# Copies of the weight sums moved from SyncE's queue to GpSimd's, each tied by a one-element transfer to a unit of the mLSTM's projection

## The chip, the cores and the metric

The kernel runs on one core of a Trainium2 chip. The core has five engines, each with its own in-order queue of instructions: PE (TensorE, matmuls), DVE (VectorE), ACT (ScalarE), POOL (GpSimd) and SP (SyncE). In this kernel SP and POOL issue all transfers, and sixteen DMA engines carry out those of both. The metric is device time in microseconds (us) of one execution.

## What is computed

One layer of a transformer-like trunk for 64 sample rows and 1024 prompt rows of width 1024, in float32:

```python
mod = silu(c) @ w_ada + b_ada                     # 48 blocks of 128 columns: shifts, scales, gates
u = rmsnorm(x, norm1_g) * (1 + sc1) + sh1
proj = u @ w_in                                   # q, k, v, mq, mk, mv, mo, gates
y_a = stick_breaking_attention(q, k, v)           # 8 heads x 64
conv = silu(depthwise_conv4(mq, mk))              # its last 3 inputs are an output, conv_new
y_b = sigmoid(mo) * norm(mlstm(conv, mv, mi, mf)) # 4 heads x 128
x = x + g1 * ((sigmoid(ga)*(y_a @ w_a) + sigmoid(gb)*(y_b @ w_b)) @ w_out)
u2 = rmsnorm(x, norm2_g) * (1 + sc2) + sh2
x = x + g2 * ((silu(u2 @ w_ff_gate) * (u2 @ w_ff_up)) @ w_ff_down)
y = rmsnorm(x, final_g)
```

## The kernel before

Every float32 operand is split into a high and a low part, and each product is three matmuls (`mm3`, lines 76 to 78). For a weight block, `w_unit` loads 128 columns (`wr`, line 64, 512 KB, on SP), and POOL makes the two parts (`hi_pool`, line 53, and `lo_pool`, line 59). `wr`, `wh` and `wl` have three buffers each.

**Start.** SP loads x and the first weights. `ada_pair(kb)` loads two blocks of `w_ada` (`wada`, line 212, ten buffers, 512 KB each), PE multiplies them (line 215) and transposes the result (line 220), and DVE makes `mod` and `A1` of it (line 238). `make_u(kb)` then scales `xnT[kb]` on ACT (line 299), POOL makes `uh` and DVE `ul`, and PE adds the slice `kb` to the first two units of the projection (`ps_mx`: mq and mk of head 0). This happens for kb = 0 to 7, so that 16 blocks of `w_ada` are needed before the first unit of the projection is done. Then come the gates' matmuls (`ps_if`, lines 573 and 574) and the units mv and mo of head 0.

**The mLSTM phase.** For each head h = 0 to 3 the list `dense` has the units q, k, v of the attention and mq, mk, mv, mo of head h + 1 (for h = 3 blocks of `w_ada` and gates in their place), and `run` weaves the steps of `mlstm(h)` between them. At the end of an mq or mk unit, `evac_x` copies six columns into the small tile `cvo` (lines 685 and 686), which is written out as `conv_new` at the end of the phase. Column b of `cvo` belongs to block b: blocks 0 to 3 are mq of heads 0 to 3, blocks 4 to 7 are mk. POOL also makes the value tiles `vst`, the mask sums of `W` (line 728), `hsq` (line 784) and the product at the end of the convolution (line 698) here.

**The weight sums.** The gate and up products of ten of the 22 blocks of the FFN use sums of quarters of `w_ff_gate` and `w_ff_up`, which are prepared in DRAM: four tensors `wsum_d[1]` to `wsum_d[4]`, each 512 x 1280. Each is made by a copy of one summand (`sum_copy`, two halves of 1280 KB, DRAM to DRAM) and an accumulating transfer of the other (`sum_add`, two halves, on POOL). Sum 2 adds sum 1, and sum 4 adds sum 2. They are read by the FFN stage (`load_pair`, line 1270).

**The order of the work.** The code runs within a framework that records all instructions with their dependences and then orders each engine's queue with its own simulated timeline: an instruction can be put ahead of those that stand before it in the program as soon as nothing that it depends on is open. Waits are semaphores, and each engine's queue is fixed at build time. A DMA that writes what an earlier DMA wrote, or reads what an engine writes, waits for it in the queue of the engine that issues it.

Of the kernel before, what the change touches and what calls it, by code (L numbers as in the profile page):

```python
# [35 lines left out]
def trunk(ctx, tc, a, o, dbg=None, stop=None):  # L36
    nc = tc.nc
# [82 lines left out]
    cvo = const.tile([P, 48], F32, name="cvo")  # L120
# [32 lines left out]
    NFC = NF * P  # L153
    wsum_d = {x: dram.tile([KH, NFC], F32, name=f"wsum{x}_d") for x in (1, 2, 3, 4)}
    g1w, g2w, u1w, u2w = w_g[0:KH, 0:NFC], w_g[KH:D, 0:NFC], w_u[0:KH, 0:NFC], w_u[KH:D, 0:NFC]
    sum_parts = {1: (u1w, u2w), 2: (g1w, wsum_d[1]), 3: (u1w, g1w), 4: (g2w, wsum_d[2])}

    def sum_copy(x):
        def go():
            for c in range(0, NFC, NFC // 2):  # L160
                nc.sync.dma_start(wsum_d[x][:, c : c + NFC // 2], sum_parts[x][0][:, c : c + NFC // 2])
            return
            yield
        return go()

    def sum_add(x):
        def go():
            for c in range(0, NFC, NFC // 2):
                nc.gpsimd.dma_start(wsum_d[x][:, c : c + NFC // 2], sum_parts[x][1][:, c : c + NFC // 2], accum_op=ALU.add)
            return  # L170
            yield
        return go()
# [644 lines left out]
    def qkv_units(p):  # L817
        return [in_unit(f"q{p}", OFF_Q + P * p, (p, 0), evac_qk, alloc_qk),
                in_unit(f"k{p}", OFF_K + P * p, (p, 1), evac_qk, alloc_qk), k_post(p),
                in_unit(f"v{p}", OFF_V + P * p, (p,), evac_v, alloc_v), v_post(p)]  # L820

    def ml_units(h):
        return [in_unit(f"mq{h}", OFF_MQ + P * h, (h, 0), evac_x, alloc_x),
                in_unit(f"mk{h}", OFF_MK + P * h, (h, 1), evac_x, alloc_x),
                in_unit(f"mv{h}", OFF_MV + P * h, (h,), evac_mv, alloc_mv),
                in_unit(f"mo{h}", OFF_MO + P * h, (h,), evac_mo, alloc_mo)]
# [8 lines left out]
    def chain(gens):  # L835
        for g in gens:
            yield from g

    def run(consumer, dense, nsteps, nd):

        n = 0.0
        done = False
        if nd == 0:
            for _ in consumer:
                pass
            done = True
        for _ in dense:
            n += nsteps / max(nd, 1)
            while n >= 1.0 and not done:
                n -= 1.0  # L850
                done = next(consumer, "end") == "end"
        for _ in consumer:
            pass
# [52 lines left out]
    for h in range(4):  # L906
        q_, k_, kp, v_, vp = qkv_units(h)
        m_ = ml_units(h + 1) if h < 3 else ada_left[0:2] + gates[0:2]
        b_ = [[sum_copy(1), sum_copy(3), sum_copy(2), sum_copy(4)], [sum_add(1), sum_add(3)], [sum_add(2)], [sum_add(4)]][h]
        dense = []  # L910
        for i, g in enumerate([q_, k_, kp, v_, vp] + m_):
            dense += [g] + (b_[i // 2 : i // 2 + 1] if i % 2 == 0 else [])
        run(mlstm(h), chain(dense), 14, 23 if h < 3 else 17)
# [99 lines left out]
    for m in range(KB):  # L1013
        if m % 2 == 0:
            wh, wl = wide_unit(w_a, 0, 4, m // 2, f"wa{m}")
        for c, (s, e) in enumerate(CHUNKS):
# [11 lines left out]
            for lo, hi in ([(s, HT), (HT, e)] if s < HT < e else [(s, e)]):  # L1028
                h = lo // HT
# [535 lines left out]
```

## Time and profile before

| | us |
|---|---|
| median of 3 runs | 1891.38 |
| lowest and highest | 1888.59 and 1891.83 |
| profiled execution | 1888.55 |
| its span | 1886.8 |
| PE busy (share of the span) | 1766.3 (94%) |
| POOL busy | 664.6 (35%) |
| mean granted clock of TensorE | 0.969 |

The span is what the profiler recorded; the profiled execution took 1.75 us more than it. A row of the timeline gives the start, the duration, the engine, the line of the code, the operation, the tile written and the tiles read, the count and, in brackets, how long the engine was idle before and what ended that. A row of the waits gives who waited for what, the total in us, how many times, and the longest. "In" tensors are the kernel's inputs in DRAM. MB and GB/s are decimal.

### The profile page before, as it was taken

What the parts mean: (1) busy time and instruction counts of PE and PEld (TensorE: products, weight loads), DVE (VectorE), ACT (ScalarE), POOL (GpSimd) and SP (SyncE); (2) the same over time, 40 slices, a digit from 0 to 9 for tenths busy, and PEclk for the clock granted to TensorE, in tenths of its full rate; (3) what the DMA queues carried; (4) which work ended last, traced back from release to release, by engine and by line L of the source; (5) the groups of instructions that cost most, each with busy time, mean ns of one, the idle gap of its engine ahead of it and who ended that gap; (6) DMA issues with size and microseconds to landing.
All of it is one profiled execution on the core that took longest, in us unless ns stands there. A gap on an engine that the chain in (4) does not pass through costs nothing. (4 is left out here: it accounts for less than half of the span.)

```text
span 1886.8 us, 31673 instructions
## 1 busy us (share of the span) xinstructions
PE 1766.3 (94%) x12388; PEld 1701.0 (90%) x12388; DVE 1000.8 (53%) x1903; ACT 670.5 (36%) x1401; POOL 664.6 (35%) x546
## 2 busy tenths in 40 slices
PE   6459999999989999997998999999999999999997
PEld 4349999999989888886898999999999999999997
DVE  5242242424236857687755198755554676444535
ACT  4023243434224444444422267433332443100005
POOL 2233353535243322249566350032222002254333
PEclk9769999999999999998999999999999999999999
DMA  9985333233485556477467345732232566443102
GB/s 273 269 218 135 98 96 106 84 118 79 132 188 136 131 136 155 128 196 218 138 205 209 106 127 159 207 108 75 69 92 75 173 203 185 170 151 116 57 12 96
DMA packets 315224, 265.51 MB, mean 141 GB/s; under 512 B 13638, under 2 KB 285250, under 8 KB 315074
## 3 DMA queue, kind: packets, MB, share of 16 engines
q1 hardware_dynamic: 305218, 235.16, 42.0%
q0 software_dynamic: 9856, 28.32, 7.3%
q8 instruction: 98, 1.61, 0.3%
q14 instruction: 52, 0.43, 0.1%
HBM read 206.59 MB, written 77.81 MB: 151 GB/s over the span
## 5 line engine op out<-in xcount | busy, mean ns | idle before, releaser
L76 PE MATMUL ps_fd<-hh,wh_fd 128*128 128x384 f32 (+1 forms) x480 | 157.1, 327 | 1.2 <-DVE hst L1333 1.2
L78 PE MATMUL ps_fd<-hh,wl_fd 128*128 128x384 f32 (+1 forms) x480 | 157.2, 327 | 0.0
L77 PE MATMUL ps_fd<-hl,wh_fd 128*128 128x384 f32 (+1 forms) x480 | 157.1, 327 | 0.0
L56 DVE TENSOR_TENSOR w<-wr,w 128x512 fp32r<-128x512 f32 x140 | 95.4, 691 | 39.4 <-ACT w L47 36.4
L1417 DVE SCALAR_TENSOR_TENSOR x1f<-ps_fd,mod,x1f 128x384 f32<-128x384 f32 (+2 forms) x128 | 60.4, 496 | 101.8 <-PE ps_fd L78 101.8
L388 DVE TENSOR_TENSOR_SCAN re<-re 128x128 f32<-128x128 f32 (+3 forms) x64 | 107.3, 1679 | 13.3 <-ACT re L384 12.9
L47 ACT CAST w<-wr 128x512 fp32r<-128x512 f32 x140 | 85.1, 619 | 69.6 <-PE ps_gd L1341 17.7
L53 POOL TENSOR_SCALAR wh_fd<-wr_fd 128x1024 fp32r<-128x1024 f32 x20 | 24.6, 1232 | 227.6 <-PE ps_ga L1341 119.4
L76 PEld LDWEIGHTS ps_fd<-hh,wh_fd 128*128 128x128 f32 x480 | 90.1, 188 | 1.4 <-POOL wl_fd L59 1.4
L78 PEld LDWEIGHTS ps_fd<-hh,wl_fd 128*128 128x128 f32 x480 | 90.1, 188 | 0.0
L77 PEld LDWEIGHTS ps_fd<-hl,wh_fd 128*128 128x128 f32 x480 | 90.1, 188 | 0.0
L47 ACT CAST hh<-hr 128x1088 fp32r<-128x1088 f32 (+1 forms) x26 | 24.0, 961 | 175.2 <-PE ps_fd L77 152.3
L384 ACT ACTIVATE re<-z 128x512 f32<-128x512 f32 (+2 forms) x96 | 47.3, 494 | 91.0 <-DVE z L380 70.6
L1341 PE MATMUL ps_ga<-b1h,w 128*128 128x272 f32 x352 | 75.0, 292 | 2.5 <-ACT g L1326 1.8
L215 PE MATMUL ps_ada<-wada,cT 128*32 128x128 f32 x768 | 43.1, 309 | 33.8 <-DMA wada<-in_w_ada 33.5
L1341 PE MATMUL ps_gc<-b5h,w 128*128 128x272 f32 x352 | 74.7, 292 | 0.0
L1341 PE MATMUL ps_gb<-b6h,w 128*128 128x272 f32 x352 | 74.4, 290 | 0.2 <-ACT g L1326 0.2
L1341 PE MATMUL ps_gd<-b7h,w 128*128 128x272 f32 x352 | 74.4, 290 | 0.0
L1341 PE MATMUL ps_gc<-b3h,w 128*128 128x272 f32 x352 | 73.7, 288 | 0.0
L1341 PE MATMUL ps_gd<-b4h,w 128*128 128x272 f32 x352 | 73.6, 289 | 0.0
L1341 PE MATMUL ps_ga<-b2h,w 128*128 128x272 f32 x352 | 73.5, 288 | 0.0
L215 PEld LDWEIGHTS ps_ada<-wada,cT 128*32 128x32 f32 x768 | 23.2, 119 | 49.5 <-issue 26.5
(549 smaller groups left out, 6108.8 us busy)
## 6 DMA issues: line engine op xcount, KB each, us to landing
wada<-in_w_ada SPq DMA_DIRECT2D x48, 512.0 KB
wr<-wsum_d SPq DMA_DIRECT2D x80, 256.0 KB
h_d<-hst SPq DMA_DIRECT2D x44, 272.0 KB
wr<-in_w_ff_gate SPq DMA_DIRECT2D x40, 256.0 KB
wr_fd<-in_w_ff_down SPq DMA_DIRECT2D x20, 512.0 KB
hr<-h_d SPq DMA_DIRECT2D x18, 544.0 KB
wr_g<-in_w_ff_gate SPq DMA_DIRECT2D x12, 512.0 KB
wr_u<-in_w_ff_up SPq DMA_DIRECT2D x12, 512.0 KB
```

The costliest lines, as they stand in the source:

```text
L47: nc.scalar.copy(out, in_)
L53: nc.gpsimd.tensor_scalar(out, in_, 1.0, 0.0, ALU.mult, ALU.add)
L56: nc.vector.tensor_sub(out, in_, h.bitcast(F32))
L76: nc.tensor.matmul(ps, wh, xh, start=first, stop=False)
L77: nc.tensor.matmul(ps, wh, xl, start=False, stop=False)
L78: nc.tensor.matmul(ps, wl, xh, start=False, stop=last)
L215: nc.tensor.matmul(ps[g : g + 32, b * P : (b + 1) * P], cT[:, kb, :], raw[:, kb, :], start=kb < 4, stop=kb >= 4, tile_position=(0, g))
L384: nc.scalar.activation(rest[:, c0 : c0 + w], ps, AF.Sigmoid, scale=-scale)
L388: nc.vector.tensor_tensor_scan(r, r, r, 1.0, ALU.mult, ALU.bypass)
L1341: nc.tensor.matmul(ps, w[:, a, j, :], b[j // 2][:, j % 2, :], start=p in (1, 6, 5, 7) and j == 0 and k == 0, stop=j == 3 and k == 2, skip_ ...
L1417: nc.vector.scalar_tensor_tensor(x1[m][:, lo:hi], ps[:, lo - s : hi - s], mod[:, 40 + m, g : g + 1], x1[m][:, lo:hi], ALU.mult, ALU.add)
```

## The change

`sum_copy` takes a second argument, a column of `cvo`. Both halves of each copy are issued by POOL instead of SP, and ahead of each half a transfer of one element (4 bytes) from that column of `cvo` goes into the first element of the place that the half fills; the half then overwrites it. Copies 1 and 3 are tied to blocks 1 and 5 (mq and mk of head 1), copies 2 and 4 to blocks 2 and 6 (mq and mk of head 2). In the program, the copies move from the units of h = 0 to those of h = 1 and 2, and the accumulating transfers stand a few units later than they did. What is computed stays the same.

```diff
-    def sum_copy(x):
+    def sum_copy(x, b):
+
         def go():
             for c in range(0, NFC, NFC // 2):
-                nc.sync.dma_start(wsum_d[x][:, c : c + NFC // 2], sum_parts[x][0][:, c : c + NFC // 2])
+                nc.gpsimd.dma_start(wsum_d[x][0:1, c : c + 1], cvo[0:1, b : b + 1])
+                nc.gpsimd.dma_start(wsum_d[x][:, c : c + NFC // 2], sum_parts[x][0][:, c : c + NFC // 2])
             return
             yield
         return go()
...
         m_ = ml_units(h + 1) if h < 3 else ada_left[0:2] + gates[0:2]
-        b_ = [[sum_copy(1), sum_copy(3), sum_copy(2), sum_copy(4)], [sum_add(1), sum_add(3)], [sum_add(2)], [sum_add(4)]][h]
+        b_ = [[], [sum_copy(1, 1), sum_copy(3, 5), sum_add(1), sum_add(3)], [sum_copy(2, 2), sum_copy(4, 6), sum_add(2)],
+              [sum_add(4)]][h]
         dense = []
         for i, g in enumerate([q_, k_, kp, v_, vp] + m_):
             dense += [g] + (b_[i // 2 : i // 2 + 1] if i % 2 == 0 else [])
```

## The prediction

> **What bounds the kernel now.** I read the forty slices of the page first, for stages in which PE is not busy.
>
> ```profile
> PE   6459999999989999997998999999999999999997
> DMA  9985333233485556477467345732232566443102
> ```
>
> PE is at 9 nearly everywhere but in the first four slices (a slice is 47 us), where the DMA engines are at 9, 9, 8. So the start is bound by transfers and the rest by PE. The busy times by window then place it.
>
> ```profile
> 40.00:61.50 21.50, 19.13 (x172) 16.19 (x171) 10.41 (x17) 5.04 (x7) 14.14 (x11) 1.00 0.99 283
> 61.50:125.50 64.00, 21.05 (x142) 17.19 (x142) 7.70 (x23) 6.20 (x13) 7.15 (x7) 0.60 1.02 254
> 125.50:160.00 34.50, 30.57 (x183) 26.01 (x181) 22.07 (x48) 12.54 (x18) 17.39 (x10) 0.95 0.82 167
> ```
>
> After start and length come PE, PEld, DVE, ACT and POOL, then PE's clock, the DMA engines' share and GB/s. From 61.5 to 125.5 PE works 21.05 of 64 us, at a clock of 0.60, with the DMA engines full. The waits of PE from 51 to 120 name what it lacks.
>
> ```profile
> PE ps_ada L215 <- DMA wada<-in_w_ada: 32.8, 5, 17.8
> PE ps_mx L76 <- POOL uh L53: 11.1, 2, 8.8
> ```
>
> 32.8 us go to blocks of `w_ada`. The timeline of SP shows why they are late.
>
> ```profile
> 40.63 1.25 SPq L161 DMA_DIRECT2D wsum_d<-in_w_ff_up  x2
> 41.97 0.60 SPq L212 DMA_DIRECT2D wada<-in_w_ada  x1
> 42.62 5.43 SPq L161 DMA_DIRECT2D wsum_d<-in_w_ff_up  x1
> 48.15 1.12 SPq L212 DMA_DIRECT2D wada<-in_w_ada  x1
> 49.31 5.87 SPq L161 DMA_DIRECT2D wsum_d<-in_w_ff_up  x1
> 55.23 27.18 SPq L161 DMA_DIRECT2D wsum_d<-in_w_ff_gate  x4
> 82.51 6.54 SPq L64 DMA_DIRECT2D wr_mo<-in_w_in  x1
> 89.15 17.69 SPq L212 DMA_DIRECT2D wada<-in_w_ada  x3
> ...
> 108.65 1.58 SPq L212 DMA_DIRECT2D wada<-in_w_ada  x1
> ```
>
> All eight copies stand in SP's queue from 40.6 us, far ahead of their place in the program: nothing held them back. Issuing them alone takes 1.25 + 5.43 + 5.87 + 27.18 = 39.7 us (the transfers push back), and the last four blocks of `w_ada` are issued only from 89 on. The 11.1 us on `uh` come from the same place, as the timelines of POOL and PE show.
>
> ```profile
> 83.25 1.00 POOL L169 DMA_DIRECT2D wsum_d<-in_w_ff_gate  x1 [22.22 <-DMA wsum_d<-in_w_ff_up]
> 83.90 1.48 POOL L53 TENSOR_SCALAR uh<-xnT 128x1088 fp32r<-128x1088 f32 x1
> 85.44 1.28 PE L76 MATMUL ps_mx<-uh,wh_mq 128*128 128x320 f32 x3 [8.76 <-POOL uh L53]
> ```
>
> POOL stood 22.22 us in front of an accumulating transfer whose copy had not landed; `uh` was behind it, and PE behind `uh`.
>
> **The change part by part.**
>
> *The copies leave SP's queue at the start.* Will they stay out of it? Each half now overwrites an element that a one-element transfer writes, and that reads a column of `cvo`. These are the copies into columns 1 and 2; columns 5 and 6, of the mk units, are written after each.
>
> ```profile
> 213.19 1.16 DVE L685 COPY cvo<-xp 128x3 f32<-128x3 f32 x1 [2.78 <-ACT xp L678]
> ...
> 310.30 1.16 DVE L685 COPY cvo<-xp 128x3 f32<-128x3 f32 x1 [2.77 <-ACT xp L678]
> ```
>
> No copy can start before 213 us of today's timeline, and no accumulating transfer before its copy. So the start loses the eight copies and, with them, accumulating transfers such as that at 83 us.
>
> Do the DMA engines still bind? The rows of SP show the last six blocks of `w_ada` (1, 1, 3 and 1). From 40 us on these six and the weights of mv, mo and q are to be moved: 9 x 512 KB = 4.72 MB, and at the 283 GB/s of the window from 40 that is 16.7 us. The last block would land at about 57 us, before 61.5, where PE ran dry. So PE is next to bind. What it has left then is worked out from these rows.
>
> ```profile
> 58.83 0.64 PE L215 MATMUL ps_ada<-wada,cT 128*32 128x128 f32 x16
> 74.37 1.08 PE L215 MATMUL ps_ada<-wada,cT 128*32 128x128 f32 x16 [12.70 <-DMA wada<-in_w_ada]
> 122.42 0.65 PE L76 MATMUL ps_mx<-uh,wh_mq 128*128 128x320 f32 x3
> 125.53 0.31 PE L573 MATMUL ps_if<-uh,wif 128*16 128x320 f32 x1
> 51.63 0.38 PE L220 MATMUL ps_ada<-ident,ada_sb 128*128 128x128 f32 x2
> 54.32 0.77 PE L76 MATMUL ps_mx<-uh,wh_mq 128*128 128x320 f32 x3 [2.31 <-POOL uh L53]
> ```
>
> Five blocks at 0.64, three pairs of transposes at 0.38 and three slices of `ps_mx` at 125.53 - 122.42 = 3.11: 3.2 + 1.1 + 9.3 = 13.6 us at the full clock, where the window has 21.05 at 0.60. Not all of that will be gapless: in the five slices before, the one gap after 43 us was 2.31 us, for `uh`. For three slices I allow 4.4 us, two such gaps less a little. The stretch of 64 us then takes 18 us, a gain of 46. Bounds: 64 - 13.6 = 50.4 with no gap, 64 - 21.05 = 43 if the clock stays low and no gap is left.
>
> On the clock the row comes first: a block costs 0.64 us at 58.8 and 1.08 after 12.7 us of idleness, and the window from 40, with a gap of 2.31, has a clock of 1.00. The Trainium skill (TensorE: Matmul & The Clock Gate, Part 1: The HAM clock gate) says that the clock halves after an idle window of about 3.4 us and needs as long a busy one to come back; by that, gaps above it would cost what the second rival below charges. The rows above agree on both sides of it.
>
> *The issues on POOL.* Eight copies and eight one-element transfers are new on POOL, and the accumulating ones only move. The nearest rows:
>
> ```profile
> L169 POOL DMA_DIRECT2D wsum_d<-wsum_d x4: 998/1013/1037, 117.3 to 144.9; - x4
> DMA to landing us min/median/max: 10.2/12.9/22.7
> L447 POOL DMA_DIRECT2D vx<-v_d x8: 519/552/582, 554.2 to 816.5; - x8
> DMA to landing us min/median/max: 2.5/3.9/9.6
> ```
>
> The second and fourth rows are the landings of the first and third. 8 x 1.01 + 8 x 0.55 = 12.5 us of POOL, in two groups from 213 and 310 on. Besides, POOL waits for each small transfer ahead of its half, and for each half ahead of its accumulating transfer. What is queued behind it are the weight conversions. How late may they be?
>
> ```profile
> 236.52 1.05 POOL L53 TENSOR_SCALAR wh_q<-wr_q 128x1024 fp32r<-128x1024 f32 x1 [10.34 <-PE ps_mk L77]
> 237.66 2.40 POOL L59 TENSOR_TENSOR wl_q<-wr_q,wh_q 128x1024 fp32r<-128x1024 f32 x1
> L76 PE MATMUL ps_q<-uh,wh_q x24: 306/334/338, 262.3 to 274.9; 128*128 128x384 f32 x16, 128*128 128x320 f32 x8
> ```
>
> The parts of q are ready at 240.06 and PE uses them at 262.3: 22.2 us of cover, and POOL idled 10.34 us before. A copy and its two small transfers, issued together, hold POOL for about 3.9 + 12.9 = 16.8 us, less than the cover. So I take 1 us for the issues and waits of all four copies. The upper end is 8.8 us, what the one such wait that was not covered cost PE (the row at 85.44); the lower is 0, since a queue that waits more gives nothing back. Without that cover it would be about 4 x 16.8 = 67 us.
>
> *The transfers in the mLSTM phase.* Eight copies and eight accumulating transfers of 1280 KB, 21 MB, now run beside the weights of the projection.
>
> ```profile
> 200.00:240.00 40.00, 40.00 (x266) 39.96 (x265) 13.53 (x28) 12.55 (x30) 15.09 (x14) 1.00 0.27 83
> 320.00:360.00 40.00, 40.00 (x257) 39.97 (x256) 21.00 (x37) 17.98 (x36) 17.61 (x17) 1.00 0.23 57
> L1270 SPq DMA_DIRECT2D wr<-wsum_d x80: 359/501/1422, 1106.2 to 1579.8; - x80
> ```
>
> PE is busy throughout there, and the DMA engines only a quarter of the time. Half of 21 MB falls on each stretch: 10.5 MB at 283 - 83 = 200 GB/s is 52 us of full engines. Today's window from 125.5 to 160, with the last of the four accumulating transfers in the row of POOL and a DMA share of 0.82, has PE busy for 30.57 of 34.5 us, so nearly full engines alone do not starve it. I take 0 for this, and the sums are first read at 1106 us.
>
> **Sum.** 46 gained, 1 given back: 45 us. The profiled execution's 1888.55 becomes 1843.5 (span 1842). The median of the runs lies 2.83 us above that execution, and I put the forecast as much higher: 1846.
>
> **The rivals.**
>
> *GpSimd's queue serializes (slower).* If POOL waited for every landing in turn, each copy would hold it for 2 x 3.9 + 2 x 12.9 = 33.6 us, 11.4 beyond the cover of 22.2; four copies cost 45.6, and the gain is just gone: that landing of 12.9 is the point from which it decides. With 20 us, nearer the maximum of 22.7, it is 47.8 per copy, 4 x 25.6 = 102 lost, and the time 1846 + 101 = 1947. For it: the wait of 22.22. Against it: the halves of a copy went out two in 1.25 us, so they don't wait for one another, and the engines are far emptier at 213 than at 60. 4 in 100.
>
> *The chain per slice binds instead of PE (a smaller gain).* From a block to `uh` the work passes PE, DVE, ACT and POOL.
>
> ```profile
> 77.12 0.23 DVE L238 TENSOR_SCALAR A<-mod,c1T 128x2 f32<-128x2 f32 x1
> 77.39 1.57 ACT L299 ACTIVATE xnT<-xnT,mod,A 128x64 f32<-128x64 f32 x2 [22.84 <-DVE A L238]
> ```
>
> From the block's end at 74.37 + 1.08 = 75.45 to ACT's end at 78.96, and 1.48 for `uh`: 5.0 us. If the three slices went through it one after the other, with the clock down, the stretch would take 21.05 + 15 = 36 us: a gain of 28, less 1, and 1864. For it: POOL also converts weights between the `uh`s (the 2.31 us gap). Against it: slices 0 to 4 overlapped. 11 in 100.
>
> *The copies stay at the start (no change).* If the tie did not bind, the same bytes would run on the same DMA engines, now from POOL: about 1891. The Trainium skill (DMA: Bandwidth & Descriptors, Issuing engines are not separate DMA queues) has it that transfers of all issuing engines run on the same 16 and interleave, so a change of queue alone frees nothing; the trace agrees, with a share of 1.02 where POOL's accumulating transfers and SP's run together. Against this rival stand the rows of `cvo`. 1 in 100.
>
> *The order elsewhere changes.* All queues are planned anew, and the plan of the mLSTM and attention phases may come out some us better or worse; nothing in the trace prices it. It widens the range by a few us, and I give 2 in 100 to a loss that eats the gain.
>
> **How the numbers follow.** The forecast has 82 in 100: 1838 (no gap, nothing given back: 1891.38 - 50.4 = 1841, and 3 us for the plan) to 1857 (43 gained and 8.8 given back). The range reaches up to the second rival: 1838 to 1864. I call 0.2% (3.8 us) the least that a measurement can tell from no change. Faster: 82 + 11, and 1 of the others: 94. Same: 2. Slower: 4.
>
> **What the profile after would show.** No row of a copy before 160 us, and all of them on POOL; SP issuing the last `wada` before 60; PE's wait for `wada` below 3 us and the first `ps_if` matmul at 75 to 85 us instead of 125.5; a clock near 1.00 there; the copies in two groups, near 165 and 265 us, with POOL waits of up to 15 us ahead of `sum_add`; and PE busy for 40 of 40 us beside them. PE waiting there for `wh` or `wl` of a unit would show the first rival, waits for `uh` of some 5 us at 60 to 90 the second. The prediction is wrong if the first `ps_if` comes after 90 us, or if PE idles over 10 us more between there and 560.

## The result, and the profile after

| | before | after |
|---|---|---|
| median of 4 runs, us | 1889.99 | 1871.31 |
| lowest and highest, us | 1887.52 and 1891.83 | 1861.14 and 1873.54 |
| profiled execution, its span, us | 1888.55, 1886.8 | 1861.14, 1859.4 |
| its mean granted clock | 0.969 | 0.979 |

The ratio after to before is 0.9891 with a 95% interval of 0.9851 to 0.9932: faster by 0.7 to 1.5%, some 20 us, where 45 were forecast; 1871 lies above the range of 1838 to 1864. The profiled execution is the fastest of the four, 27.4 us of span below before.

The forty slices after (46.5 us each; before they were 47.2) show that the change has two sides.

```profile
PE   6899799999989999988998999999999999999997
DMA  9427749423485565684566345622222666443102
```

At the start, the second and third slice have risen from 4 and 5 to 8 and 9; the fifth and the eighth have fallen from 9 to 7. The first side in detail, by windows from 40 us to the first `ps_if` matmul (start and length, PE, PEld, DVE, ACT, POOL, clock, DMA share, GB/s), before and then after, with that matmul's row of the timeline after:

```profile
40.00:125.50 85.50, 40.18 (x313) 33.37 (x313) 18.11 (x40) 11.24 (x20) 21.29 (x18) 0.70 1.01 261
```

```profile
40.00:70.80 30.80, 29.80 (x285) 25.63 (x283) 16.23 (x38) 11.11 (x19) 12.16 (x11) 1.00 0.69 175
```

```profile
70.77 0.39 PE L575 MATMUL ps_if<-uh,wif 128*16 128x320 f32 x1
```

`ps_if` starts at 70.8 instead of 125.5: 54.7 us gained. PE is idle 1.0 us there instead of 45.3 and, at the full clock, busy 29.8 instead of 40.2. SP's queue after, with the last six blocks of `w_ada`, all issued before 53 us:

```profile
39.38 2.76 SPq L214 DMA_DIRECT2D wada<-in_w_ada  x2
42.23 1.53 SPq L64 DMA_DIRECT2D wr_mo<-in_w_in  x1
43.85 5.08 SPq L214 DMA_DIRECT2D wada<-in_w_ada  x3
...
51.06 1.69 SPq L214 DMA_DIRECT2D wada<-in_w_ada  x1
```

The other side is the mLSTM phase. The rows of the mo units (four heads; behind the durations stand the first and last start in us), before and after:

```profile
L76 PE MATMUL ps_mo<-uh,wh_mo x96: 302/334/346, 153.2 to 456.1; 128*128 128x384 f32 x64, 128*128 128x320 f32 x32
```

```profile
L76 PE MATMUL ps_mo<-uh,wh_mo x96: 302/334/442, 97.6 to 428.0; 128*128 128x384 f32 x64, 128*128 128x320 f32 x32
```

The first is 55.6 us earlier, the last only 28.1: the phase takes 330.4 us instead of 302.9 and gives back 27.5. What remains at its end, 28 us, is what the span has won; later stages hardly change it (27.4 us of span). The windows of the phase and the waits of PE from 200 to 240, after:

```profile
160.00:200.00 40.00, 40.00 (x259) 39.97 (x258) 19.10 (x33) 9.35 (x20) 19.43 (x21) 1.00 0.97 265
200.00:240.00 40.00, 28.13 (x152) 27.34 (x151) 8.08 (x19) 16.21 (x27) 20.71 (x18) 0.83 0.62 142
280.00:320.00 40.00, 40.00 (x256) 39.88 (x254) 17.48 (x31) 9.90 (x19) 20.17 (x15) 1.00 1.00 261
320.00:360.00 40.00, 32.70 (x180) 31.04 (x179) 9.79 (x24) 20.04 (x37) 16.52 (x16) 0.87 0.54 142
```

```profile
PE ps_q L76 <- POOL W L730: 8.6, 1, 8.6
PE ps_yb L799 <- DVE hn L790: 3.3, 1, 3.3
```

PE is idle 11.9 and 7.3 us in the second and fourth window and runs at 0.83 and 0.87 of its clock there. These two windows follow the two in which the sums' transfers fill the DMA engines, with shares of 0.97 and 1.00.

The copies run on POOL, from 163 and 276 us on, near the 165 and 265 forecast (rows of the small transfers and of the copies, and below each kind the time from issue to landing):

```profile
L162 POOL DMA_DIRECT2D wsum_d<-cvo x8: 521/539/759, 159.6 to 287.4; - x8
DMA to landing us min/median/max: 2.4/6.3/10.1
L163 POOL DMA_DIRECT2D wsum_d<-in_w_ff_up x4: 636/652/704, 163.4 to 184.8; - x4
L163 POOL DMA_DIRECT2D wsum_d<-in_w_ff_gate x4: 634/649/691, 276.3 to 297.9; - x4
DMA to landing us min/median/max: 7.0/10.6/13.3
```

What does `ps_q` wait for? The profile names POOL's work on W, and W leads to a load that the prediction never looked at: `W<-nm_d` (576 KB), issued by SP only when the last reader of the W before has ended (at 191.86 us for head 1), for W has one buffer. Its issue and the first use of W on DVE, `dc`, for head 1 before, and then for heads 1 and 2 after:

```profile
246.01 0.37 SPq L723 DMA_DIRECT2D W<-nm_d  x1
252.83 1.15 DVE L725 TENSOR_TENSOR dc<-W,mcb 128x8 f32<-128x8 f32 x1 [1.28 <-DMA W<-nm_d]
```

```profile
191.88 0.37 SPq L725 DMA_DIRECT2D W<-nm_d  x1
213.59 0.18 DVE L727 TENSOR_TENSOR dc<-W,mcb 128x8 f32<-128x8 f32 x1 [15.60 <-DMA W<-nm_d]
303.80 0.53 SPq L725 DMA_DIRECT2D W<-nm_d  x1
321.11 0.17 DVE L727 TENSOR_TENSOR dc<-W,mcb 128x8 f32<-128x8 f32 x1 [10.29 <-DMA W<-nm_d]
```

From issue to use it took 6.8 us, and takes 21.7 and 17.3 now. Each engine works through its queue in order, so much stands behind `dc`, as ACT's and PE's timelines after show.

```profile
213.87 0.21 ACT L731 ACTIVATE dc<-dc 128x9 f32<-128x9 f32 x1 [17.94 <-DVE dc L728]
215.39 0.44 ACT L713 ACTIVATE mog<-ps_mo 128x320 f32<-128x320 f32 x1
215.97 0.60 PE L76 MATMUL ps_q<-uh,wh_q 128*128 128x320 f32 x1 [8.59 <-POOL W L730]
```

ACT stands 17.94 us in front of `dc`. Behind `dc` it has to empty the banks of the finished mo unit (`mog`); PE has three banks of PSUM for the units, all three hold mo, and `ps_q` starts 0.14 us after the first is emptied at 215.83. POOL's work on W, which the wait names, was let go by the same `dc`: POOL had stood 8.74 us in front of it. Either way the wait leads to the same load.

### The profile page after: what moved, and what is told of

The parts are those of the page before. It is cut to its first block, busy times and chain, and to the rows that moved or that the text cites. A ratio compares the mean times of both kernels' runs of the same rounds, so it can differ in the third digit from the quotient of the medians.

```text
span 1859.4 us, 31695 instructions
## 1 busy us (share of the span) xinstructions
PE 1763.3 (95%) x12388; PEld 1695.7 (91%) x12388; DVE 995.4 (54%) x1903; ACT 673.5 (36%) x1403; POOL 678.2 (36%) x562
## 5 line engine op out<-in xcount | busy, mean ns | idle before, releaser
L76 PE MATMUL ps_ga<-uh,wh_ga 128*128 128x384 f32 (+1 forms) x192 | 64.9, 338 | 1.5 <-DVE re L388 1.1
L56 DVE TENSOR_TENSOR al<-ps_a,ah 128x512 fp32r<-128x512 f32 (+1 forms) x80 | 49.4, 629 | 30.3 <-ACT ah L47 30.1
```

What stands on the lines that cost most here:

```text
L56: nc.vector.tensor_sub(out, in_, h.bitcast(F32))
L76: nc.tensor.matmul(ps, wh, xh, start=first, stop=False)
```

## The experiments

Theory L: that load lands late because the sums fill the DMA engines. Theory Q: POOL's own waits for landings are what costs. Each edit is against the changed kernel unless said otherwise; ratios are to the kernel before, with 95% intervals.

**Without any sums.**

```diff
-        b_ = [[], [sum_copy(1, 1), sum_copy(3, 5), sum_add(1), sum_add(3)], [sum_copy(2, 2), sum_copy(4, 6), sum_add(2)],
-              [sum_add(4)]][h]
+        b_ = [[], [], [], []][h]
...
-        src = {1: half(w_g, 0), 6: half(wsum_d[2], 0), 5: half(wsum_d[1], 0), 7: half(wsum_d[3], 0),
-               2: half(w_g, 1), 3: half(wsum_d[4], 0), 4: half(w_u, 1)}
+        src = {1: half(w_g, 0), 6: half(w_g, 0), 5: half(w_u, 0), 7: half(w_g, 1),
+               2: half(w_g, 1), 3: half(w_u, 1), 4: half(w_u, 1)}
```

> The weight sums are left out of the changed kernel: no small transfer, no copy, no accumulating transfer; the FFN reads quarters of the weights of the same size in their place, so its products are others. What is left is the start without the copies. If the whole give-back of 27 us in the mLSTM phase comes from the sums (all theories of it agree), the first ps_if starts near 71 us, PE is busy throughout from 160 to 360, and the time is about 1871 - 27 - a few = 1834 to 1845. If part of the give-back comes from the new order of the queues, the time stays above 1850.

Measured: 1842.14 us, ratio 0.9746 (0.9727 to 0.9766). `ps_if` starts at 73.3, and PE is busy for 40.00 of 40 us in each window from 160 to 360. The row of the mo units:

```profile
L76 PE MATMUL ps_mo<-uh,wh_mo x96: 302/334/443, 100.2 to 403.6; 128*128 128x384 f32 x64, 128*128 128x320 f32 x32
```

The phase takes 303.4 us, against 302.9 before. So the sums cause the whole give-back; the planner's new order does not.

**Two buffers for W.** The load of a head's W can then be issued one head earlier; the sums stay as they are. The other lines make room for it: the gates get one staging tile less, and two small output tiles take the places of others.

```diff
-        W = slot([P, 9, P], f"W{h}", "W")
+        W = slot([P, 9, P], f"W{h}", "W", 2)
...
-    cur["d"], cur["gt"] = 3, 2
+    cur["d"], cur["gt"] = 3, 1
...
-    st_o = small([48, P], "cv_o", "cv_o", bufs=1)
+    st_o = small([48, P], "cv_o", "g9", bufs=1)
-    st_n = small([8, P], "n_o", "n_o", bufs=1)
+    st_n = small([8, P], "n_o", "g8", bufs=1)
```

> The changed kernel with two buffers for W in place of one (and, for the space, one buffer for a gate's staging tile in the mLSTM phase), so that SP can issue the load of W for a head one head earlier. Theory L (the late load): the load of W, issued just before it is used, lands after 21.7 us instead of 6.8 because the copies fill the DMA engines; DVE, ACT and POOL stand behind it in order, and PE runs out of PSUM banks. Then the wait for W goes, PE is busy for 40 of 40 us from 200 to 240 and 320 to 360, and the time falls to 1838 to 1850. Theory Q (POOL's queue: its waits for landings delay the weight parts and hsq): POOL's waits stay as they are, and the time stays at 1865 to 1875.

Measured: 1838.47 us (1836.86 to 1842.37), ratio 0.9737 (0.9721 to 0.9753). Its windows and its row of the mo units:

```profile
160.00:200.00 40.00, 40.00 (x258) 39.97 (x257) 18.33 (x36) 11.78 (x26) 19.51 (x21) 1.00 0.97 267
200.00:240.00 40.00, 39.07 (x243) 37.61 (x242) 13.10 (x24) 17.77 (x34) 24.63 (x20) 1.00 0.73 183
280.00:320.00 40.00, 37.95 (x240) 37.53 (x238) 20.75 (x36) 20.62 (x34) 24.12 (x22) 1.00 1.07 247
320.00:360.00 40.00, 40.00 (x262) 38.88 (x261) 6.41 (x18) 12.12 (x34) 14.15 (x11) 1.00 0.43 133
```

```profile
L76 PE MATMUL ps_mo<-uh,wh_mo x96: 302/334/443, 97.9 to 404.4; 128*128 128x384 f32 x64, 128*128 128x320 f32 x32
```

The DMA engines are as full (0.97 and 1.07), but PE is idle for only 3.0 us in these windows, and the clock stays at 1.00. The phase takes 306.5 us: 3.6 given back instead of 27.5. The waits of POOL from 150 to 240, in the changed kernel and then in this one:

```profile
POOL wsum_d L171 <- DMA wsum_d<-in_w_ff_up: 8.6, 3, 4.8
POOL wsum_d L163 <- DMA wsum_d<-cvo: 6.9, 1, 6.9
```

```profile
POOL wsum_d L171 <- DMA wsum_d<-in_w_ff_up: 8.4, 3, 5.1
POOL wsum_d L163 <- DMA wsum_d<-cvo: 7.0, 1, 7.0
```

POOL waits as before and it costs next to nothing: theory Q falls, theory L stands.

**The control: two buffers for W in the kernel before.** The same edit, with the copies on SP and untied.

> The control: the kernel before (copies on SP, untied) with two buffers for W. There the load of W lands in 6.8 us and PE is busy for 40 of 40 us in the mLSTM phase, so theory L expects no gain: 1884 to 1892. If two buffers for W help by themselves, whatever the copies do, the time falls by 10 us or more.

Measured: 1887.91 us, ratio 0.9998 (0.9988 to 1.0008). The buffer is worth nothing where the load is not crowded.

**The ties left out.**

```diff
-                nc.gpsimd.dma_start(wsum_d[x][0:1, c : c + 1], cvo[0:1, b : b + 1])
```

> The changed kernel without the eight one-element transfers: copies on POOL, but nothing holds them back. If the gain at the start comes from the time at which the copies run (both theories), they run at the start again and the time is 1885 to 1905, with PE waiting 30 us or more for wada. If the change of the issuing queue alone freed SP and so brought part of it, the time would be below 1880.

Measured: 1909.09 us, ratio 1.0115 (1.0096 to 1.0133): slower than before, and the expectation's upper end missed by 4 us. The copies now start at once, and POOL's first weights come late:

```profile
1.38 2.11 POOL L162 DMA_DIRECT2D wsum_d<-in_w_ff_up  x3 [0.37 <-issue]
...
4.94 2.47 POOL L162 DMA_DIRECT2D wsum_d<-in_w_ff_gate  x4
...
76.25 1.04 POOL L53 TENSOR_SCALAR wh_mq<-wr_mq 128x1024 fp32r<-128x1024 f32 x1 [48.82 <-DMA wr_mq<-in_w_in]
```

Before, that first conversion (`wh_mq`) ran at 23.76 us. In SP's queue the copies stood behind the first weights; in POOL's, nothing is ahead of them. So the tie brings the gain, and the change of queue without it loses 21 us. The Trainium skill (DMA: Bandwidth & Descriptors, Issuing engines are not separate DMA queues) says that the transfers of all issuing engines run on the same 16 DMA engines and interleave; this run agrees, for copies in POOL's queue put the weights of SP's off by some 52 us, and it adds that a queue with nothing in it lets a transfer start sooner than is good.

**The accumulating transfers left out.**

```diff
-        b_ = [[], [sum_copy(1, 1), sum_copy(3, 5), sum_add(1), sum_add(3)], [sum_copy(2, 2), sum_copy(4, 6), sum_add(2)],
-              [sum_add(4)]][h]
+        b_ = [[], [sum_copy(1, 1), sum_copy(3, 5)], [sum_copy(2, 2), sum_copy(4, 6)],
+              []][h]
```

> The accumulating transfers are left out of the changed kernel (wsum holds only the copied summand, so the FFN's products are others); ties, copies and the single buffer of W stay. POOL loses its waits ahead of sum_add, and half of the bytes go. Theory L (the load of W lands late because the engines are full): the second copy of each pair still runs from 184 on, against the load at about 192, so the load lands in 8 to 14 us instead of 21.7, PE's wait shrinks but need not vanish, and the time is 1842 to 1856. If the accumulating transfers alone filled the engines, the time is that without any sums, 1842, with a load of about 7 us.

Measured: 1841.59 us, ratio 0.9754 (0.9739 to 0.9768): a hair below the expected range, and the time of the kernel without sums. Load and use of W for head 1, and the window in which the load runs, here and then in the changed kernel:

```profile
192.07 0.37 SPq L725 DMA_DIRECT2D W<-nm_d  x1
198.17 1.89 DVE L727 TENSOR_TENSOR dc<-W,mcb 128x8 f32<-128x8 f32 x1 [0.55 <-DMA W<-nm_d]
```

```profile
190.00:200.00 10.00, 10.00 (x66) 10.00 (x66) 3.76 (x13) 1.68 (x4) 3.44 (x2) 1.00 0.27 74
```

```profile
190.00:200.00 10.00, 10.00 (x67) 9.96 (x66) 4.34 (x14) 1.68 (x4) 2.63 (x3) 1.00 1.00 295
```

With half the bytes the engines are nearly empty from 190 on (0.27 against 1.00), and the load takes 6.1 us. The copies had ended by then, which I had not expected. It takes the sums' whole length to reach the load. (POOL's waits ahead of `sum_add` are gone too, so this run by itself does not tell the two theories apart.)

**Small transfers and copies on SP, with the ties.** In `sum_copy`, `nc.sync` in place of `nc.gpsimd`, twice.

> The changed kernel with the small transfers and the copies on SP's queue instead of POOL's; the accumulating ones stay on POOL. Theory L: the gain at the start is the same (first ps_if at 70 to 75), for it comes from the tie; in the mLSTM phase SP now stands in front of copies that wait for the small transfers, with the load of W and the weights behind them, so the give-back is the same or larger: 1865 to 1890. If POOL's queue were what costs, the time falls below 1855.

Measured: 1877.19 us, ratio 0.9942 (0.9924 to 0.996). `ps_if` starts at 72.9. In SP's queue and on DVE:

```profile
177.87 0.53 SPq L162 DMA_DIRECT2D wsum_d<-cvo  x2
189.80 1.17 SPq L163 DMA_DIRECT2D wsum_d<-in_w_ff_up  x2
...
193.07 2.88 SPq L725 DMA_DIRECT2D W<-nm_d  x1
218.75 0.17 DVE L727 TENSOR_TENSOR dc<-W,mcb 128x8 f32<-128x8 f32 x1 [18.61 <-DMA W<-nm_d]
```

The load now stands in the same queue behind two halves of a copy and one load of weights and takes 25.7 us; PE idles 16.3 us in the window from 200 to 240 instead of 11.9. The start's gain is nearly that of POOL's queue, the give-back larger.

**Earlier ties.** Copies 1 and 3 tied to head 0's mq and mk, copy 2 to head 1's mq and copy 4 to head 2's.

```diff
-        b_ = [[], [sum_copy(1, 1), sum_copy(3, 5), sum_add(1), sum_add(3)], [sum_copy(2, 2), sum_copy(4, 6), sum_add(2)],
-              [sum_add(4)]][h]
+        b_ = [[sum_copy(1, 0), sum_copy(3, 4), sum_add(1), sum_add(3)], [sum_copy(2, 1), sum_add(2)], [sum_copy(4, 2), sum_add(4)],
+              []][h]
```

> The changed kernel with other ties: copies 1 and 3 tied to blocks 0 and 4 (mq and mk of head 0, written near 70 us), copy 2 to block 1 and copy 4 to block 2, so that the first two run from 70 us on, where the DMA engines stand at a share of 0.04 to 0.21, and then only one copy runs ahead of each load of W. Theory L: the first two sums end before or near the load of W at 115, a single sum (copy and accumulating transfer, about 25 us from 158) ends before the load of W at 192, and the time is 1835 to 1850. Theory Q: POOL has the same number of waits, and the give-back stays above 15 us: 1855 to 1872.

Measured: 1844.37 us, ratio 0.9769 (0.9753 to 0.9786), as L expects. The loads of W for heads 1 and 2 and their uses:

```profile
200.40 0.37 SPq L725 DMA_DIRECT2D W<-nm_d  x1
207.78 0.60 DVE L727 TENSOR_TENSOR dc<-W,mcb 128x8 f32<-128x8 f32 x1 [1.84 <-DMA W<-nm_d]
297.48 0.37 SPq L725 DMA_DIRECT2D W<-nm_d  x1
303.56 1.90 DVE L727 TENSOR_TENSOR dc<-W,mcb 128x8 f32<-128x8 f32 x1 [0.53 <-DMA W<-nm_d]
```

7.4 and 6.1 us, with PE busy throughout from 160 to 360. But PE waited 4.91 us for a state tile at 82 us, against 2.22 in the changed kernel. That the two sums, which now run from 70 us on, crowd its small load is likely, but was not shown.

**One sum at a time**, with two buffers for W (the edit above) and with one. Copies 1, 3, 2 and 4 are tied to head 0's mk and to the mq of heads 1, 2 and 3.

```diff
-        b_ = [[], [sum_copy(1, 1), sum_copy(3, 5), sum_add(1), sum_add(3)], [sum_copy(2, 2), sum_copy(4, 6), sum_add(2)],
-              [sum_add(4)]][h]
+        b_ = [[sum_copy(1, 4), sum_add(1)], [sum_copy(3, 1), sum_add(3)], [sum_copy(2, 2), sum_add(2)], [sum_copy(4, 3), sum_add(4)]][h]
```

> The changed kernel with two buffers for W and the four sums spread over the phase: copies 1, 3, 2, 4 tied to blocks 4, 1, 2 and 3 (near 70, 158, 255 and 350 us), each followed by its accumulating transfers. With the load of W out of the way, PE has only 3 us left to win between 160 and 360, so theory L expects 1833 to 1845, no different from the kernel with two buffers alone (1838.5) beyond the scatter.

> The changed kernel with one buffer for W, as it was, and the four sums spread: copies 1, 3, 2, 4 tied to blocks 4, 1, 2 and 3. With two buffers for W this order left the DMA engines at a share of 0.29 from 190 to 200, where the load of W is issued. Theory L: the load lands in about 7 us without a second buffer, no give-back is left, and the time is 1832 to 1842. If the second buffer is needed all the same, the time is above 1850.

Measured: with two buffers 1833.59 us (1831.75 to 1834.78), ratio 0.9713 (0.9697 to 0.9729); with one 1835.07 (1834.27 to 1838.12), ratio 0.9716 (0.9699 to 0.9732). The second buffer is not needed when the load finds room: it takes 6.4 us.

```profile
195.39 0.37 SPq L725 DMA_DIRECT2D W<-nm_d  x1
201.75 1.62 DVE L727 TENSOR_TENSOR dc<-W,mcb 128x8 f32<-128x8 f32 x1 [0.81 <-DMA W<-nm_d]
```

Both are the fastest kernels here, 54.7 and 53.6 us below before. That with two buffers is also 5 us below the two buffers with the old ties, which I had not expected; PE is idle 3 us less from 160 to 360 there, and its last mo unit starts 3.5 us earlier, which is most of the 3.9 us between the two spans.

**The changed kernel again.**

> The changed kernel once more. Its runs went from 1861 to 1874, wider than any other kernel here, and the profile at hand is that of the fastest. Theory L: the scatter is that of the landing of W under full engines. A profile of 1869 or more shows landings longer than the 21.7 and 17.3 us of the first one and PE's waits near 200 to 240 and 320 to 360 longer by about the difference, with the first ps_if again at 70 to 72. If the scatter comes from another stage, those waits are as before.

Measured: 1858.52 us (1853.58 to 1870.16), ratio 0.985 (0.9813 to 0.9887). The profile is of a run of 1856, with loads of 20.2 and 18.7 us, where one of 1869 or more was wanted. The phase gives back 25.7 us in it, so the give-back is there again. But it does not bear out that the scatter of this kernel, 1854 to 1874 over eight runs, is that of the crowded load: its span is 5.0 us shorter than the first profile's, while its last mo unit starts only 1.2 us earlier. Most of the difference arises behind the phase, ahead of the first `ps_wo` matmul (977.2 instead of 982.8 us). The cause of the scatter stays open; the kernels in which the load is free keep within 8 us.

## Why the prediction was wrong, point by point

- *What bounds the start, and that the tie holds*: right. No copy starts before 163 us, `w_ada` is no longer waited for, and without the ties the gain is gone. It was 54.7 us instead of 46, and above the upper bound of 50.4. From 40 us on I had reckoned 6.8 us of idle PE (2.4 up to 61.5, and 4.4 allowed behind it), where it was 1.0; and 32.7 us of work, where it was 29.8, for the new order has some of the start's work done before 40 (285 matmuls from 40 on instead of 313). That is 5.8 + 2.9 = 8.7 us of luck, which hid part of the failed step below.
- *The issues and waits on POOL, 1 us*: right in effect. POOL waited 6.9 + 8.6 = 15.5 us for its own transfers in the first group, less than the 16.8 I reckoned for each of its two copies, and the run with two buffers for W shows that these waits cost next to nothing.
- *The transfers in the mLSTM phase, 0 us*: this is the step that failed. They cost 27.5 us, idle PE and lower clock together, and made the sum 54.7 - 27.5 = 27 us instead of 45. I worked out myself that the engines would be full for about 52 us per group, and then excused it with a window (125.5 to 160) in which they were nearly full and PE busy. But that window holds no load of W: the first is issued at 169.1 us. The cover of 22.2 us, which I read for the weights, does not hold for W: the row of DVE before shows 1.28 us of waiting for a load issued 6.8 us ahead, so it had no slack at all.
- *GpSimd's queue serializes*: did not happen. PE waited for no `wh` or `wl` of a unit there. This rival charged the right stretch with the wrong queue.
- *The chain per slice binds*: did not happen; the one wait for `uh` left was 0.87 us.
- *The copies stay at the start*: tried by leaving the ties out. Its price was wrong: 1909 instead of 1891.
- *The order elsewhere changes*: hardly. Without any sums the mLSTM phase takes 303.4 us against 302.9, and from the last mo unit to the first `ps_wo` it is 552.3 us before, 554.8 and 550.4 in the two profiles after.
- *The signs*: the first `ps_if` came early enough, but the second sign of being wrong came true. From the first `ps_if` to 560 us PE idles 29.8 us, where it idled 8.9.
- *PE's lower clock*: the two stalls cost more than their idle time. PE's idle time in the two windows is 11.9 + 7.3 = 19.2 of the 27.5 us; the clock of 0.83 and 0.87 there is the likely rest. PE was busy there for 60.8 us with 332 matmuls, which at the 260 in 40 us of the window from 240 would be 51 (an estimate, for the shapes differ). The window behind the stall of 8.6 us, after:

```profile
210.00:220.00 10.00, 4.03 (x15) 4.06 (x16) 2.08 (x5) 6.05 (x10) 6.07 (x11) 0.52 0.77 159
```

The rule of the Trainium skill that the prediction quoted (TensorE: Matmul & The Clock Gate, Part 1: The HAM clock gate) would have halved the clock after a stall of 8.6 us, and the trace agrees, with 0.52.

## What to carry to other kernels

When a transfer is moved to a stretch in which PE is busy and the DMA engines idle, list the loads of that stretch that are issued only when their single buffer comes free: here they had no cover, whatever cover the weights had, and engines that work in order carried the delay to PE. Look for them among the small waits of every engine, not among PE's alone: here a wait of 1.28 us on DVE was the mark of one that grew to 15.6 beside the traffic. Then either give that tile a second buffer or space the moved transfers so that each group ends before the next such load; here each won back nearly all that the change had lost.

## What the runs showed of the hardware

- 576 KB of W (rows of 512 bytes) take 6.1 to 8.1 us from issue to use with the DMA engines partly free, and 17.3 to 21.7 us beside transfers of 1280 KB from the other queue: about two and a half to three times as long.
- A transfer of 4 bytes lands in 2.4 us at best, and in 10.1 at most. One issued at 174 us, with copies of the same queue under way, was awaited by POOL until 184.
- Moved to a queue with nothing ahead of them, untied copies started at 1.4 us and put off the first conversion of weights from 24 to 76 us. In SP's queue, behind the first weights, the untied copies had started at 40.6.
